# Decoder layer kernel: the residual stream in two halves that share their places with the weight buffers, and operands handed over mid-way

## The chip, the cores and the metric

The kernel runs on one core of a Trainium2 chip. The metric is the device time of one execution in microseconds (us). Five engines run side by side, each with its own queue: TensorE (PE, matmuls; its weight loads are shown as PEld), VectorE (DVE), ScalarE (ACT), GpSimd (POOL) and SyncE (SP, which here issues most DMAs; ACT issues the others).

## The reference

One decoder layer on 512 tokens of width 2048, in float32. A normalised input is projected for two groups of heads that work in parallel, a gated DeltaNet and a latent attention. Their outputs are concatenated, and the rest is what matters here:

```python
x = x + mixed @ w_out[l]
h = rms_norm(x, ffn_norm_w[l])
x = x + (jax.nn.silu(h @ w_gate[l]) * (h @ w_up[l])) @ w_down[l]
return rms_norm(x, final_norm_w)
```

`w_out` is 2048 x 2048, `w_gate` and `w_up` are 2048 x 5632, `w_down` is 5632 x 2048.

## The kernel before

Tokens are kept in four tiles of 128 partitions. Every matmul operand in float32 is split into a rounded high part and a low part (`hi` and `lo`), and `mm3` (L143) issues three matmuls for a product: high by high, high by low, low by high. `load_w` (L117) fetches a piece of weights, 512 KB, into one of two `raw` buffers on SP's queue, lets ACT cast it into `whi` (L137) and DVE subtract into `wlo` (L138); `whi` and `wlo` have three buffers each, unless the caller gives a destination of its own.

**Output projection.** `out_part` (L717) adds 512 columns of `mixed @ w_out` for four heads to `x2`, the residual stream (128 partitions x 4 token tiles x 2048 columns, 32 KB per partition): two `load_w`, then per token tile 12 matmuls of 512 columns and DVE's addition (L726). The last four calls (L889 to L894) also let ACT sum the squares of `x2` (L728), write `x2` to DRAM (`x2d`), and prepare what the next phase reads.

**Operands of the tokens.** `operands(i)` (L873) transposes 256 columns of `x2` on PE (8 transposes into two `bank` tiles of PSUM, L878), scales them on ACT (L882 to L884) into `stg`, of which there is one buffer, forms four differences on DVE (L886), and splits all seven into `ch` and `cl` (ACT L284, DVE L285). It runs eight times: 0 and 1 after block 1 of the last output projection, and so on, 6 and 7 at the end. Then the mean square is turned into `rstd` (POOL's power, L170), and `rows_of` (L239) spreads it over all partitions with matmuls (L150) into `rbc`.

**Gate and up.** For 22 pairs of feature tiles `unit` (L912) computes 256 columns of a product with 2048 inputs by Strassen-Winograd: seven `product`s of 24 matmuls of 256 columns each, once for `w_gate` and once for `w_up`. Its 2 MB of weights come by four DMAs into one of two `wraw` buffers (L916); DVE forms sums of their quarters (L927; three of them per unit in `raw` buffers, one in `sw`), and each product's weights are split into `whi` and `wlo`. The result `silu(gate) * up` goes to DRAM (`actd`), in 11 groups of four feature tiles.

**Down.** For each group g, `act_group(g)` (L982) loads its activations back by two `load_w` into `ah` and `al` (two buffers each), and `down` (L1002) adds four column blocks of 512 to `x2b` (L1012): two `load_w` and 48 matmuls of 512 columns per block. `act_group(g + 1)` is called ahead of `down(g)`. The last group runs by token tile instead, with its weights held in `fh` and `fl`, so that the final normalisation and the output can follow. Its DMAs for `x2b` (L999, 4 MB) and the final gain (L1000) are issued by ACT.

**Order and places.** Each engine runs its own instructions in the order emitted. The framework takes them in program order among those that are ready in its own model of the run, and puts in the waits. Tiles live in pools; a new tile waits for the last use of the tile whose slot it takes, or whose bytes lie under it after a pool was closed. Pools stack from two sides of the memory. On the right, `wr` (the `wraw` buffers) and `gu` (the results of units) open where `x2` and the operands of the output projection were, and reach far enough to lie over the closed pool `tr` of the left side (`stg`, `jo`); `ad` (`ah`, `al`) opens where `wr` was. `banks` (L99) does the same for the eight PSUM banks.

Of the kernel before, what the change touches and what calls it, by code (L numbers as in the profile page):

```python
# [89 lines left out]
def layer_kernel(ctx: ExitStack, tc: tile.TileContext, x, positions, w_in, a_log, dt_bias, w_uq, w_ukv,  # L90
# [605 lines left out]
    banks(op=1, score=3, acc=2, bank=2)  # L696
    x2_stack = right.enter_context(ExitStack())
    x2 = pool(x2_stack, "x2", side="right").tile([P, NT, D], F32, name="x2")
    mix_right = right.enter_context(ExitStack())
# [5 lines left out]
    for c in range(4):  # L705
        nc.scalar.dma_start(x2[:, :, c * S:(c + 1) * S], xv[:, :, c * S:(c + 1) * S])

# [8 lines left out]

    def out_part(k0, mg, c, jo=None):  # L717
        cs = slice(c * S, (c + 1) * S)
        ws = [load_w(w_out_v[:, k0 + 2 * kk:k0 + 2 * kk + 2, cs], 2, S) for kk in range(2)]
        for t4 in range(NT):  # L720
            sl = slice(t4 * P, (t4 + 1) * P)
            a = acc()
            for k in range(4):
                wh, wl = ws[k // 2]
                mm3(a, mg[0][:, k, sl], mg[1][:, k, sl], wh[:, k % 2, :], wl[:, k % 2, :], k == 0, k == 3)
            nc.vector.tensor_tensor(out=x2[:, t4, cs], in0=a, in1=x2[:, t4, cs], op=ALU.add)  # L726
            if jo is not None:
                nc.scalar.activation(jo, x2[:, t4, cs], AF.Square, accum_out=ssx[:, t4, c:c + 1])  # L728

# [143 lines left out]
    def operands(i):  # L873
        tps = []
        for k in (2 * i, 2 * i + 1):
            tp = bank()
            for t4 in range(NT):
                nc.tensor.transpose(tp[:, t4 * P:(t4 + 1) * P], x2[:, t4, k * P:(k + 1) * P], ident)  # L878
            tps.append(tp)
        st = tr.tile([P, N7, H], F32, name="stg", tag="stg", bufs=1)  # L880
        wa, wb = fw[:, 2 * i:2 * i + 1], fw[:, 2 * i + 1:2 * i + 2]
        nc.scalar.mul(st[:, 0, :], tps[0][:, 0:H], wa)  # L882
        nc.scalar.mul(st[:, 5, :], tps[0][:, H:S], wa)
        nc.scalar.mul(st[:, 1:3, :].rearrange("p a n -> p (a n)"), tps[1], wb)  # L884
        for o, x, y in ((3, 5, 0), (5, 2, 5), (4, 2, 3), (6, 1, 4)):
            nc.vector.tensor_tensor(out=st[:, o, :], in0=st[:, x, :], in1=st[:, y, :], op=ALU.subtract)  # L886
        split(ch[:, :, i, :], cl[:, :, i, :], st)

    for c in range(4):  # L889
        out_part(12, mg_b, c, jo)  # L890
        nc.scalar.dma_start(x2d[c].rearrange("p (t n) -> p t n", t=NT), x2[:, :, c * S:(c + 1) * S])
        if c:
            operands(2 * c - 2)
            operands(2 * c - 1)  # L894
# [5 lines left out]
    rsq(rstd, st4[:, 0:4])  # L900
    rows_of(tr, rstd, rbc, "jo")
    mix_right.close()
    x2_stack.close()
    tr_stack.close()
# [3 lines left out]
    gu = pool(gu_right, "gu", side="right")  # L908
    wr_right = right.enter_context(ExitStack())
    wr = pool(wr_right, "wr", bufs=2, side="right")  # L910
# [52 lines left out]

    for u in range(NFF // 2):
        g, o = divmod(u, 2)
        s = gu.tile([P, 2, S], F32, name="sg", tag="sg", bufs=2)
        unit(wg_v, u * 2 * P, s)
        nc.vector.tensor_tensor(out=s, in0=s, op=ALU.mult,
                                in1=rbc.rearrange("p (o n) -> p o n", o=1).broadcast_to([P, 2, S]))
        nc.scalar.activation(s, s, AF.Silu)  # L970
        t = gu.tile([P, 2, S], F32, name="up", tag="up")
        unit(wu_v, u * 2 * P, t)
        nc.vector.tensor_tensor(out=s, in0=t, in1=s, op=ALU.mult)
        nc.scalar.dma_start(actd[g].rearrange("p (k n) -> p k n", n=S)[:, 2 * o:2 * o + 2, :], s)


    wr_right.close()
    banks(bank=8)
    ad_right = right.enter_context(ExitStack())
    ad = pool(ad_right, "ad", bufs=2, side="right")  # L980
# [9 lines left out]

    cur = act_group(0)
    cb_stack.close()
# [21 lines left out]

    for g in range(NG - 1):
        nxt = act_group(g + 1)
        down(g, *cur)
        cur = nxt
    prev = cur
# [69 lines left out]
```

## Time and profile before

| What | Value |
|---|---|
| Time, median of 3 runs | 2510.67 us (2506.42 to 2512.49) |
| Profiled execution: its own time | 2509.5 us |
| Profiled execution: span from first to last instruction | 2507.7 us |
| PE busy | 2345.4 us, 94% of the span |
| DVE, ACT busy | 1565.9 us (62%), 899.6 us (36%) |
| Mean granted TensorE clock | 0.965 of full |
| Moved by DMA | 257.69 MB, mean 103 GB/s |

A duration of a matmul in the profile includes the time in which the next one already runs; the distance of two starts is what one costs. The order in time is output projection with operands up to about 1005 us, gate and up until 1905.6 us, down projection after that. A releaser, where one is shown, is what ended an engine's idle time, as far as the profile tells.

### The profile page before, as it was taken

Reading aid. Unit: us, or ns where it says so; the run is one execution under the profiler, and the core shown is the slowest. Engines: PE = TensorE matmul, PEld = TensorE weight load, DVE = VectorE, ACT = ScalarE, POOL = GpSimd, SP = SyncE. Lnnn points to the kernel's source line nnn. Section 1 sums busy time; section 2 is a strip of 40 time slices with the busy share of each in tenths; the row PEclk is TensorE's granted clock in tenths of the full one; section 3 lists DMA queues with packets and bytes.
Section 4 is the critical chain, followed back from the end, with each engine's and each line's share of the span. In section 5 each row is a group of like instructions: output and inputs, shape, how many; then the busy total and the mean of one; then the engine's idle time right before and its main releaser. Section 6 shows DMA issues by size and latency. Waiting matters only on the chain.

```text
span 2507.7 us, 35015 instructions
## 1 busy us (share of the span) xinstructions
PE 2345.4 (94%) x14310; PEld 2067.5 (82%) x14310; DVE 1565.9 (62%) x2248; ACT 899.6 (36%) x1435; POOL 83.4 (3%) x89
## 2 busy tenths in 40 slices
PE   8999999999999996799999999999997888788888
PEld 6778877777777785799999999999996777677776
DVE  6656565654655556677777777777774444444446
ACT  5333333332332335344444444444442111211123
POOL 0011111100000000000000000000000000000000
PEclk9999999999999997899999999999998999899999
DMA  5222322222322222433333333333335322333333
GB/s 172 78 71 81 83 79 78 76 77 69 129 80 72 64 69 82 143 110 118 110 119 122 130 118 119 119 110 118 110 118 181 95 94 92 101 109 101 94 100 118
DMA packets 210401, 257.69 MB, mean 103 GB/s; under 512 B 18112, under 2 KB 162752, under 8 KB 210112
## 3 DMA queue, kind: packets, MB, share of 16 engines
q1 hardware_dynamic: 197920, 225.55, 29.1%
q10 hardware_dynamic: 12320, 29.90, 3.3%
q8 instruction: 112, 1.84, 0.3%
q14 instruction: 49, 0.40, 0.1%
HBM read 235.23 MB, written 20.19 MB: 102 GB/s over the span
## 4 chain that ended last, share of the span: by engine, by line
PE 81%; DVE 7%; DMA 5%; ACT 3%; issue 2%; POOL 1%; ACTq 0%; SPq 0%; POOLq 0%; DVEq 0%
PE x L147 7%; PE x L145 7%; PE x L146 7%; PE acc L146 7%; PE acc L147 7%; PE acc L145 7%; PE bank L145 6%; PE bank L146 6%; PE bank L147 6%; PE bank L150 4%; PE y L147 3%; PE y L146 3%; PE y L145 3%; DMA raw<-in_w_down 2%; PE z L145 2%
## 5 line engine op out<-in xcount | busy, mean ns | idle before, releaser
L137 ACT CAST whi<-raw 128x1024 fp32r<-128x1024 f32 (+1 forms) x210 | 218.2, 1039 | 578.4 <-PE bank L147 233.5
L145 PE MATMUL x<-ch,whi 128*128 128x256 f32 x1408 | 399.4, 284 | 14.1 <-ACT whi L284 14.1
L146 PE MATMUL x<-cl,whi 128*128 128x256 f32 x1408 | 399.1, 283 | 0.0
L147 PE MATMUL x<-ch,wlo 128*128 128x256 f32 x1408 | 399.1, 283 | 0.0
L138 DVE TENSOR_TENSOR wlo<-raw,whi 128x1024 fp32r<-128x1024 f32 (+1 forms) x210 | 253.4, 1208 | 194.4 <-ACT whi L137 193.8
L145 PE MATMUL bank<-whi,ah 128*128 128x512 f32 x640 | 260.2, 410 | 80.4 <-ACT whi L137 80.4
L145 PEld LDWEIGHTS x<-ch,whi 128*128 128x128 f32 x1408 | 271.1, 193 | 14.5 <-ACT whi L284 14.4
L146 PEld LDWEIGHTS x<-cl,whi 128*128 128x128 f32 x1408 | 271.1, 193 | 0.0
L147 PEld LDWEIGHTS x<-ch,wlo 128*128 128x128 f32 x1408 | 271.0, 192 | 0.0
L146 PE MATMUL acc<-hl,whi 128*128 128x512 f32 (+1 forms) x656 | 263.7, 402 | 0.0
L145 PE MATMUL acc<-hh,whi 128*128 128x512 f32 (+1 forms) x656 | 261.7, 399 | 1.8 <-ACT whi L137 1.8
L147 PE MATMUL acc<-hh,wlo 128*128 128x512 f32 (+1 forms) x656 | 263.1, 401 | 0.0
L146 PE MATMUL bank<-wlo,ah 128*128 128x512 f32 x640 | 260.1, 406 | 0.4
L147 PE MATMUL bank<-whi,al 128*128 128x512 f32 x640 | 257.0, 402 | 0.0
L1012 DVE SCALAR_TENSOR_TENSOR x2b<-bank,rstd,x2b 128x512 f32<-128x512 f32 x160 | 119.9, 750 | 189.8 <-PE bank L147 189.8
L284 ACT CAST whi<-wraw 128x1024 fp32r<-128x1024 f32 x132 | 138.3, 1048 | 221.8 <-PE y L146 143.9
L145 PEld LDWEIGHTS bank<-whi,ah 128*128 128x128 f32 x640 | 125.7, 199 | 110.9 <-ACT whi L137 84.8
L284 ACT CAST whi<-raw 128x1024 fp32r<-128x1024 f32 x132 | 138.5, 1050 | 200.2 <-PE x L146 152.4
L146 PE MATMUL y<-cl,whi 128*128 128x256 f32 x704 | 199.2, 283 | 0.0
L147 PE MATMUL y<-ch,wlo 128*128 128x256 f32 x704 | 199.2, 283 | 0.0
L145 PE MATMUL y<-ch,whi 128*128 128x256 f32 x704 | 199.2, 283 | 0.0
L285 DVE TENSOR_TENSOR wlo<-wraw,whi 128x1024 fp32r<-128x1024 f32 x132 | 161.4, 1223 | 44.7 <-ACT whi L284 44.7
(320 smaller groups left out, 4478.5 us busy)
## 6 DMA issues: line engine op xcount, KB each, us to landing
wraw<-in_w_gate SPq DMA_DIRECT2D x88, 512.0 KB, 5.8
wraw<-in_w_up SPq DMA_DIRECT2D x88, 512.0 KB, 5.6
raw<-in_w_down SPq DMA_DIRECT2D x88, 512.0 KB, 3.8
raw<-in_w_in SPq DMA_DIRECT2D x80, 512.0 KB, 3.7
raw<-in_w_out SPq DMA_DIRECT2D x32, 512.0 KB, 3.8
actd<-sg ACTq DMA_DIRECT2D x22, 512.0 KB, 2.6
raw<-actd SPq DMA_DIRECT2D x22, 512.0 KB, 3.7
rep<-dr ACTq DMA_DIRECT2D x8, 512.0 KB
```

The lines of the kernel that those rows point to most:

```text
L137: nc.scalar.copy(hi[:, :k * n], raw[:, :k * n])
L138: nc.vector.tensor_tensor(out=lo[:, :k * n], in0=raw[:, :k * n], in1=hi[:, :k * n].bitcast(F32), op=ALU.subtract)
L145: nc.tensor.matmul(ps, lhsT=lh, rhs=rh, start=start, stop=False, skip_group_check=further)
L146: nc.tensor.matmul(ps, lhsT=lh, rhs=rl, start=False, stop=False, skip_group_check=further)
L147: nc.tensor.matmul(ps, lhsT=ll, rhs=rh, start=False, stop=stop, skip_group_check=further)
L150: nc.tensor.matmul(ps, lhsT=l, rhs=r, start=start, stop=stop)
L284: nc.scalar.copy(dst_h, src)
L285: nc.vector.tensor_tensor(out=dst_l, in0=src, in1=dst_h.bitcast(F32), op=ALU.subtract)
L1012: nc.vector.scalar_tensor_tensor(out=x2[:, t4, cs], in0=a, scalar=rstd[:, t4:t4 + 1], in1=x2[:, t4, cs], op0=ALU.mult, op1=ALU.add)
```

## The change

- `x2` becomes two tiles `x2h` of 1024 columns, 16 KB per partition each, in a pool `big` with two slots, `b0` and `b1`. `x2s` picks the right half for a slice of columns.
- These slots go on to hold the weights of `unit`: the gate units' in `b0`, the up units' in `b1`. The pool `wr` is gone.
- Then they hold the activations: `act_group(g)` takes one tile with `ah` and `al` in slot `b0` or `b1` by the parity of g. The pool `ad` is gone.
- `act_group(0)` is called ahead of the last up unit, `act_group(g + 1)` inside `down(g)` after two of its four blocks.
- `operands(2c - 2)` is called half-way through block c of the last output projection, after two of four token tiles, and `operands(2c - 1)` after the block as before.
- `rows_of` for `rbc` moves from before the first gate unit to behind it, with its temporary in `gu`.
- `gu` is closed ahead of the down projection.

```diff
-    x2 = pool(x2_stack, "x2", side="right").tile([P, NT, D], F32, name="x2")
+    big = pool(right, "big", side="right")
+    x2h = [big.tile([P, NT, D // 2], F32, name=f"x2{h}", tag=f"b{h}") for h in range(2)]
...
-            nc.vector.tensor_tensor(out=x2[:, t4, cs], in0=a, in1=x2[:, t4, cs], op=ALU.add)
+            xs2 = x2s(t4, cs)
+            nc.vector.tensor_tensor(out=xs2, in0=a, in1=xs2, op=ALU.add)
             if jo is not None:
-                nc.scalar.activation(jo, x2[:, t4, cs], AF.Square, accum_out=ssx[:, t4, c:c + 1])
+                nc.scalar.activation(jo, xs2, AF.Square, accum_out=ssx[:, t4, c:c + 1])
+            if t4 == 1 and halfway is not None:
+                halfway()
...
     for c in range(4):
-        out_part(12, mg_b, c, jo)
+        out_part(12, mg_b, c, jo, (lambda: operands(2 * c - 2)) if c else None)
...
         if c:
-            operands(2 * c - 2)
             operands(2 * c - 1)
     operands(6)
     operands(7)
...
-    rows_of(tr, rstd, rbc, "jo")
...
-    def unit(w_v, c0, dst):
-
-        raw = wr.tile([P, KD, 2 * P], F32, name="wraw", tag="wraw")
+    def unit(w_v, c0, dst, buf):
+
+        raw = big.tile([P, KD, 2 * P], F32, name="wraw", tag=buf)
...
     def act_group(g):
-        ah = ad.tile([P, 4, S], F32R, name="ah", tag="ah")
-        al = ad.tile([P, 4, S], F32R, name="al", tag="al")
+        a = big.tile([P, 2, 4, S], F32R, name="ag", tag=f"b{g % 2}")
+        ah, al = a[:, 0], a[:, 1]
...
-    cur = act_group(0)
+    for u in range(NFF // 2):
+        g, o = divmod(u, 2)
+        s = gu.tile([P, 2, S], F32, name="sg", tag="sg", bufs=2)
+        unit(wg_v, u * 2 * P, s, "b0")
+        if u == 0:
+            rows_of(gu, rstd, rbc, "dg")
...
+        t = gu.tile([P, 2, S], F32, name="up", tag="up")
+        if u == NFF // 2 - 1:
+            cur = act_group(0)
+        unit(wu_v, u * 2 * P, t, "b1")
...
     def down(g, ah, al):
+        nxt = None
         for c in range(4):
+            if c == 2:
+                nxt = act_group(g + 1)
...
+        return nxt
 
     for g in range(NG - 1):
-        nxt = act_group(g + 1)
-        down(g, *cur)
-        cur = nxt
+        cur = down(g, *cur)
```

## Rows read from the trace of the kernel before

**Rows 1.** The page, part 2: busy tenths in 40 equal slices of the span.

```profile
PE   8999999999999996799999999999997888788888
...
PEclk9999999999999997899999999999998999899999
```

**Rows 2.** Busy time by stretch: length; PE, PEld, DVE, ACT, POOL; clock, DMA share, GB/s.

```profile
972.00:1017.00 45.00, 10.44 (x45) 7.86 (x43) 22.82 (x36) 18.11 (x24) 1.01 (x1) 0.54 0.30 100
1017.00:1905.56 888.56, 888.56 (x7390) 888.38 (x7390) 686.07 (x660) 392.79 (x507) 0.00 (x0) 1.00 0.35 116
1905.56:1937.80 32.24, 15.86 (x51) 11.98 (x50) 9.62 (x10) 6.29 (x8) 0.00 (x0) 0.68 0.75 267
1970.20:2023.87 53.67, 46.53 (x193) 37.54 (x192) 23.59 (x26) 10.40 (x11) 0.00 (x0) 0.90 0.31 98
```

**Rows 3.** Waits from 1905 to 2508 us: total us, times, longest us.

```profile
ACT ah L137 <- PE bank L146: 98.6, 9, 11.0
...
PE bank L145 <- ACT whi L137: 80.4, 11, 11.2
```

**Rows 4.** Timeline of ACT, down projection: start, duration, operation [idle before <- releaser].

```profile
1970.21 1.99 ACT L137 CAST ah<-raw 128x1024 fp32r<-128x1024 f32 x2 [10.96 <-PE bank L146]
1976.40 1.04 ACT L137 CAST whi<-raw 128x1024 fp32r<-128x1024 f32 x1 [4.20 <-DMA raw<-in_w_down]
...
2000.97 1.05 ACT L137 CAST whi<-raw 128x1024 fp32r<-128x1024 f32 x1 [8.46 <-PE bank L147]
...
2011.85 1.05 ACT L137 CAST whi<-raw 128x1024 fp32r<-128x1024 f32 x1 [8.46 <-PE bank L147]
...
2398.83 1.99 ACT L137 CAST ah<-raw 128x1024 fp32r<-128x1024 f32 x2 [10.96 <-PE bank L146]
```

**Rows 5.** Timeline of PE after a group of the down projection.

```profile
1977.50 1.22 PE L145 MATMUL bank<-whi,ah 128*128 128x512 f32 x2 [7.10 <-ACT whi L137]
```

**Rows 6.** DMA landing of raw (after 1880 us) and of x2b.

```profile
DMA to landing us min/median/max: 3.5/3.7/9.2
...
DMA to landing us min/median/max: 9.4/12.5/15.5
```

**Rows 7.** Timeline of DVE around the last gate unit.

```profile
1873.48 1.22 DVE L927 TENSOR_TENSOR raw<-wraw 128x1024 f32<-128x1024 f32 x1
...
1875.88 1.22 DVE L285 TENSOR_TENSOR wlo<-raw,whi 128x1024 fp32r<-128x1024 f32 x1
```

**Rows 8.** Timelines of PE, ACT and SP where the down projection begins.

```profile
1916.92 1.65 PE L145 MATMUL bank<-whi,ah 128*128 128x512 f32 x3 [11.20 <-ACT whi L137]
...
1937.79 1.06 ACT L137 CAST whi<-raw 128x1024 fp32r<-128x1024 f32 x1 [0.30 <-PE bank L147]
...
1893.57 9.54 SPq L135 DMA_DIRECT2D raw<-actd  x4
```

**Rows 9.** Timelines of ACT, DVE and SP ahead of the first gate unit.

```profile
998.96 0.47 ACT L882 ACTIVATE stg<-bank,vec 128x256 f32<-128x256 f32 x1 [2.15 <-DVE cl L285]
...
1014.91 2.00 ACT L284 CAST whi<-wraw 128x1024 fp32r<-128x1024 f32 x2 [11.52 <-DMA wraw<-in_w_gate]
...
1003.43 2.02 DVE L285 TENSOR_TENSOR cl<-stg,ch 128x1792 fp32r<-128x1792 f32 x1 [0.78 <-ACT ch L284]
...
1005.84 2.02 SPq L916 DMA_DIRECT2D wraw<-in_w_gate  x4
```

**Rows 10.** Timeline of PE from the output projection to the first gate unit.

```profile
946.67 1.03 PE L878 MATMUL bank<-fst,x 128*128 128x128 f32 x8
...
953.12 0.60 PE L878 MATMUL bank<-fst,x 128*128 128x128 f32 x4
...
1016.01 0.58 PE L145 MATMUL x<-ch,whi 128*128 128x256 f32 x1 [14.09 <-ACT whi L284]
...
1021.45 0.28 PE L147 MATMUL z<-ch,wlo 128*128 128x256 f32 x1
```

**Rows 11.** Groups by line, 972 to 1017 us: count, busy us, mean ns, idle before.

```profile
L150 PE MATMUL bank<-dg,cst 128*128 128x128 f32 x8 | 2.1, 441 | 4.6 <-ACT stg L883 4.6
```

More of the change, by code (lines that the diff above doesn't have):

```diff
@@ L696, in layer_kernel, with x2s @@
     banks(op=1, score=3, acc=2, bank=2)
-    x2_stack = right.enter_context(ExitStack())
-    x2 = pool(x2_stack, "x2", side="right").tile([P, NT, D], F32, name="x2")
+    big = pool(right, "big", side="right")
+    x2h = [big.tile([P, NT, D // 2], F32, name=f"x2{h}", tag=f"b{h}") for h in range(2)]
+    def x2s(t, k):
+        h = k.start // (D // 2)
+        return x2h[h][:, t, k.start - h * (D // 2):k.stop - h * (D // 2)]
+    every = slice(0, NT)
     mix_right = right.enter_context(ExitStack())
@@ L705, in layer_kernel @@
     for c in range(4):
-        nc.scalar.dma_start(x2[:, :, c * S:(c + 1) * S], xv[:, :, c * S:(c + 1) * S])
+        nc.scalar.dma_start(x2s(every, slice(c * S, (c + 1) * S)), xv[:, :, c * S:(c + 1) * S])
     def mix_group(slot):
@@ L715, in gdn_group, with out_part @@
         return mh, ml
-    def out_part(k0, mg, c, jo=None):
+    def out_part(k0, mg, c, jo=None, halfway=None):
         cs = slice(c * S, (c + 1) * S)
@@ L877, in operands @@
             for t4 in range(NT):
-                nc.tensor.transpose(tp[:, t4 * P:(t4 + 1) * P], x2[:, t4, k * P:(k + 1) * P], ident)
+                nc.tensor.transpose(tp[:, t4 * P:(t4 + 1) * P], x2s(t4, slice(k * P, (k + 1) * P)), ident)
             tps.append(tp)
@@ L889, in layer_kernel @@
     for c in range(4):
-        out_part(12, mg_b, c, jo)
-        nc.scalar.dma_start(x2d[c].rearrange("p (t n) -> p t n", t=NT), x2[:, :, c * S:(c + 1) * S])
+        out_part(12, mg_b, c, jo, (lambda: operands(2 * c - 2)) if c else None)
+        nc.scalar.dma_start(x2d[c].rearrange("p (t n) -> p t n", t=NT),
+                            x2s(every, slice(c * S, (c + 1) * S)))
         if c:
-            operands(2 * c - 2)
             operands(2 * c - 1)
@@ L900, in layer_kernel @@
     rsq(rstd, st4[:, 0:4])
-    rows_of(tr, rstd, rbc, "jo")
     mix_right.close()
-    x2_stack.close()
     tr_stack.close()
@@ L908, in layer_kernel @@
     gu = pool(gu_right, "gu", side="right")
-    wr_right = right.enter_context(ExitStack())
-    wr = pool(wr_right, "wr", bufs=2, side="right")
-    def unit(w_v, c0, dst):
-        raw = wr.tile([P, KD, 2 * P], F32, name="wraw", tag="wraw")
+    def unit(w_v, c0, dst, buf):
+        raw = big.tile([P, KD, 2 * P], F32, name="wraw", tag=buf)
         for kk in range(4):
@@ L962, in unit @@
         nc.scalar.copy(dst[:, 1, 0:H], X)
[L964 to L980, printed above, removed]
     def act_group(g):
-        ah = ad.tile([P, 4, S], F32R, name="ah", tag="ah")
-        al = ad.tile([P, 4, S], F32R, name="al", tag="al")
+        a = big.tile([P, 2, 4, S], F32R, name="ag", tag=f"b{g % 2}")
+        ah, al = a[:, 0], a[:, 1]
         v = actd[g].rearrange("p (k n) -> p k n", n=S)
@@ L989, in act_group @@
         return ah, al
-    cur = act_group(0)
+    for u in range(NFF // 2):
[4 more added lines that the diff above has]
+            rows_of(gu, rstd, rbc, "dg")
+        nc.vector.tensor_tensor(out=s, in0=s, op=ALU.mult,
+                                in1=rbc.rearrange("p (o n) -> p o n", o=1).broadcast_to([P, 2, S]))
+        nc.scalar.activation(s, s, AF.Silu)
+        t = gu.tile([P, 2, S], F32, name="up", tag="up")
+        if u == NFF // 2 - 1:
+            cur = act_group(0)
+        unit(wu_v, u * 2 * P, t, "b1")
+        nc.vector.tensor_tensor(out=s, in0=t, in1=s, op=ALU.mult)
+        nc.scalar.dma_start(actd[g].rearrange("p (k n) -> p k n", n=S)[:, 2 * o:2 * o + 2, :], s)
+    banks(bank=8)
+    gu_right.close()
     cb_stack.close()
```

## The prediction

> **What bounds the kernel now.** The page's 40 slices come first [rows 1]: PE is at 9 tenths nearly everywhere, with two kinds of holes, slices 16 and 17 and then the last ten at 7 to 8 tenths, and the granted clock dips in four of these. So TensorE is the bound, and only what opens a gap in it matters. The busy time by stretch [rows 2] separates the stages that the change touches. From 972 to 1017 us PE has 10.4 of 45 us of work; from 1017 to 1905.6 it is full at clock 1.00 (7390 matmuls in 888.6 us, 0.120 us each); from 1905.6 to 1937.8 it has half; and one group of the down projection (1970.2 to 2023.9) leaves 7 of 53.7 us idle, at a mean granted clock of 0.90, that is, a part of it at 1.2 instead of 2.4 GHz.
>
> The waits name the last of these [rows 3]. Nine times ACT's cast into ah waits for PE, 98.6 us in all, and PE in turn waits for ACT's whi, 80.4 us in 11 waits. ACT's timeline shows the circle [rows 4]: act_group(g+1) stands ahead of down(g), and its ah is the buffer that down(g-1) reads to its last matmul. Until then its two loads keep both raw buffers, so no weight of the new group can be loaded. After the casts at 1970.21 comes a weight load, its cast at 1976.40, and PE starts at 1977.50 after 7.10 us of nothing [rows 5].
>
> **The down projection, the main term.** Within a group a column block takes 2011.85 - 2000.97 = 10.88 us [rows 4], 48 matmuls without a gap, so four are 43.52 us. From the first cast into ah after a group to the ninth is 2398.83 - 1970.21 = 428.62 us, eight groups of 53.58 us [rows 4]. Each boundary costs 10.06 us: 7.1 us of idleness and 2.9 us because PE then runs at its low clock for a while. With nine boundaries that is 90.5 us. The change fetches act_group(g+1) after two blocks of down(g), into the place of group g-1, which by then has been dead for about 22 us, so the casts wait for nothing but their own data.
>
> What takes its place? The same ten loads per group, two of them now between blocks 1 and 2. A raw buffer is busy for one landing, a cast and a subtraction: about 3.7 us [rows 6] + 1.05 us [rows 4] + 1.2 us [rows 7], some 6.2 us with the hand-offs. Two buffers and ten loads make 5 x 6.2 = 31 us, less than the 43.5 us of matmuls. Followed through a group that starts at T: act loads land at about T+6 and T+12 (one raw buffer is held until T+11.8 by a weight that waits for its whi), block 2's weights at T+15.5 and T+18. Block 2 starts at T+21.8. If the raw buffers alternate strictly, the last of these slips to T+21.5 and PE waits some 0.7 us. I bound the new mid-group cost between 0 and 7 us over nine groups (more is a rival) and take 3, nearer to 0 because the first reading leaves 3 to 5 us of slack. The last group's weights keep their time: what comes before them is ten loads either way.
>
> **Into the down projection.** The last product of the last unit ends at 1905.56, PE starts again at 1916.92 after 11.20 us [rows 8], waits a second time, and ends block 0 at 1937.79, where the cast into its freed whi starts [rows 8]; without gaps it would end at 1905.56 + 10.88 = 1916.44. That is 21.3 us lost. Four act loads stood in the raw buffers ahead of the first weights; SP spread them over 9.5 us from 1893.57 [rows 8]. Now the two of act_group(0) go before the last up unit and those of act_group(1) after block 1, so the first weights take those early raw places, are cast by about 1903, and PE goes straight on. Left over: the 4 MB of x2b, which land 9.4 to 15.5 us after issue [rows 6] and are issued by ACT in one piece, ahead of casts, at the same point as before. Block 1's second weight and block 2's weights, behind act_group(1), pay for that. I estimate 8 us lost, so a gain of 13.3, with bounds of 6 (block 2 waits as long as PE did at first, and the clock falls) and 21 (no wait).
>
> **Into the gate and up phase.** The chain of operands(0) to (7) has one stg buffer and alternates between ACT and DVE; the last runs from 998.96 to 1003.43 + 2.02 = 1005.45 [rows 9]. Then SP issues the first gate weights (1005.84), ACT gets them at 1014.91 [rows 9], PE starts at 1016.01 and, slow at first, is through product 1 at 1021.45 [rows 10]. The weights waited for places that the operands' temporaries and x2 occupy. In the new kernel the first gate unit's buffer is the half of x2 with columns 0 to 1023, free after operands(3), and its 2 MB land while operands(4) to (7) run; SP has nothing else to issue there. Its first cast and subtraction fit into ACT's and DVE's pauses in that chain. What remains is the chain, and it starts earlier: operands(0)'s transposes come at 946.67, right behind block 1's matmuls [rows 10]; half a block earlier is 5.4 us. Work queued behind them, the adds and squares of the block's other half, has a PE 30 us ahead of the chain's end to hide behind. So operands(7) ends near 1000 us, and product 1 ends three matmuls later, at about 1000.7. Product 2 then loses some 2 us to the low clock. Against 1021.45 that is 18 us. Bounds: 9 (no earlier start, casts only after operands(7)) and 21 (all of it, no low clock); I take 18, since each step has its cover in the rows.
>
> **The rest.** rows_of now stands between unit 0's halves: 2.1 us for its 8 matmuls in the low-clock stretch [rows 11], about 1 us at full clock, on PE's path, where before PE was idle anyway: +1. Its DVE work, and the squares and x2 copies through other views, have the same sizes as before: 0, hidden by PE. In the last up unit the act loads hold both raw buffers until the gate unit's last split; but the sums that need them are made early. The first of them ran at 1873.48 [rows 7], while its first use, product 3, starts at 1905.56 - 5 x 24 x 0.120 = 1891.2. Some 10 us later is still in time: 0.
>
> **The SP queue there.** In program order act_group(0)'s loads come ahead of the last up unit's weights. SP's row shows that a load that waits for raw holds the queue: four issues in 9.5 us [rows 8]. I still take 0, since the emitted order is not the program's: four transposes of operands(1), which lack a bank, appear at 953.12 with the next block's matmuls moved ahead of them [rows 10], and the up weights' buffer is free a whole unit ahead, long before a raw one is. The Trainium skill, "DMA: Bandwidth & Descriptors", section on the anatomy of one DMA, says that a DMA's semaphore wait happens on the issuing sequencer, before dispatch. By that rule alone, in program order, the weights would come late, and the sum would be 5 us smaller; it is a rival below.
>
> **Sum.** -90.5 + 3 - 13.3 - 18 + 1 = -117.8 us. The profiled execution took 2509.5 us, a span of 2507.7 and 1.8 around it, 1.2 under the median of the runs (2510.67). On the median: 2393 us.
>
> **Rivals.**
> (a) A new gap at block 2 of every group: both raw buffers are held when its weights are due. A gap of 3 us in nine groups is 27 us, so about 2417; if the clock falls each time (2.9 us more), 2443. For it: every whi waits for a raw buffer. Against: 31 us of raw work in 43.5. 14%.
> (b) The start brings only 9 us, because casts and sums put into the operand chain delay it, or the scheduler starts operands(0) no earlier: 2402. 10%.
> (c) The queue: SP keeps program order at the last up unit. The second act load issues when a raw is freed, at 1877.1 by the subtraction that frees it [rows 7], some 8 us before that unit's first product (1885.4), and 2 MB take 9.1 us (1005.84 to 1014.91, [rows 9]), so product 1 and its lo part come late by 5 us: 2398. This is the rule of the page named above. 10%.
> (d) The hand-over does not come loose, because the shared place counts as free only late: the boundaries stay, and only the two ends gain: 2393 + 87.5 = 2480. Against: the place was last read a group earlier. 2%.
> (e) Slower: the raw ring becomes the bound. If loads that follow each other closely land like the slowest one seen, 9.2 us instead of 3.7 [rows 6], a group takes 5 x (9.2 + 2.4) = 58 us instead of 53.6, 40 us over nine groups; with the ends gaining nothing under the same slow loads the time is 2550. It decides from a landing of about 8.3 us on. Against: 9.2 occurred beside the x2b loads, and one group moves only 98 GB/s [rows 2]. 3%.
> The forecast keeps 60%, and 1% lies where amounts cancel.
>
> **Numbers.** A measurement of this kernel can tell 0.3%, some 7.5 us, from no change. Faster by more: the forecast, (a) to (d), 96%; slower 3%; same 1%. The range takes the bounds of the sum's terms and (b), (c) and the milder half of (a): 2376 (start 21, entry 21, mid-group 0, and a little beyond) to 2426.
>
> **What would show it.** Right: the nine waits of ACT's ah for PE gone, groups of 43.5 to 44.5 us at clock near 1.00, first gate weights issued before 975, PE's first product done near 1001, PE idle under 2 us at the end of the last unit. Wrong: a PE wait for whi at a block other than 0 in every group, the first unit after 1008, or a gap at about the start of the last up unit. The forecast as a whole falls if the group period stays above 48 us.

## The result and the profile after

The changed kernel takes 2398.23 us (median; 2395.82 to 2402.94) where the kernel before takes 2510.57 us on the same chip (2506.42 to 2512.49): a ratio of 0.9557, 95% interval [0.9538, 0.9576], 112 us or 4.4% faster. Forecast were 2393 us, with a range of 2376 to 2426.

The profiled execution took 2397.31 us, with a span of 2395.5 us (2507.7 before) and a mean granted clock of 0.987 (0.965). PE is busy for 2320.1 us, 97% of the span (94%). The page's slices, to be laid beside [rows 1]:

```profile
PE   8999999999999999699999999999999999999998
...
PEclk9999999999999999799999999999999999999999
```

The holes of the last ten slices are gone, and of slices 16 and 17 one is left. Busy time by stretch, with the columns of [rows 2]: the start of gate and up, gate and up, the first group of the down projection, and a later group.

```profile
972.00:1017.00 45.00, 25.46 (x112) 21.44 (x111) 30.01 (x43) 21.92 (x30) 1.01 (x1) 0.71 0.28 93
1017.00:1897.58 880.58, 880.58 (x7334) 880.44 (x7334) 680.39 (x655) 391.73 (x504) 0.00 (x0) 1.00 0.35 117
1897.58:1948.93 51.35, 46.70 (x195) 37.76 (x194) 22.77 (x26) 10.78 (x11) 0.00 (x0) 0.93 0.62 215
1980.21:2023.73 43.52, 43.52 (x193) 36.04 (x192) 23.23 (x26) 10.54 (x10) 0.00 (x0) 1.00 0.39 121
```

PE fills the whole group at clock 1.00; before, a group took 53.6 us, at 0.90. Two holes remain: PE has 25.5 of 45 us of work at the start, and 46.7 of 51.4 us in the first group. ACT's timeline in the down projection, against [rows 4]:

```profile
1980.21 1.05 ACT L137 CAST whi<-raw 128x1024 fp32r<-128x1024 f32 x1 [7.67 <-PE bank L147]
...
1999.86 1.05 ACT L137 CAST ag<-raw 128x1024 fp32r<-128x1024 f32 x1 [6.36 <-DMA raw<-actd]
...
2005.92 1.05 ACT L137 CAST ag<-raw 128x1024 fp32r<-128x1024 f32 x1 [2.90 <-DMA raw<-actd]
...
2023.73 1.05 ACT L137 CAST whi<-raw 128x1024 fp32r<-128x1024 f32 x1 [7.63 <-PE bank L147]
```

The period is 2023.73 - 1980.21 = 43.52 us, four blocks of 10.88. The casts into the activations' place (`ag`, `ah` before) no longer wait for PE, but for their own data, while PE runs on. The waits from 1897 us to the end show it in sum, against [rows 3]:

```profile
ACT whi L137 <- PE bank L147: 189.3, 55, 8.5
ACT ag L137 <- DMA raw<-actd: 90.7, 20, 7.0
```

90.7 us of waiting, about what the nine waits for PE made before, and after the first group none of it is on PE's path: ACT has nothing to do in that time.

**Where the 112.2 us of span went.** Four marks in each trace give the parts: U, the start of DVE's last addition of block 0 in the last output projection (936.89 before, 938.93 after); DVE's sum `sg<-x,p` in unit 0, which says that PE is past its first products (1033.00, 1025.03); the end of the last product of the last unit (1905.56, 1897.58); the end of group 0 of the down projection.

| Part | forecast, us | traces, us |
|---|---|---|
| up to U, not touched by the change (scatter, see below) | 0 | +2.0 |
| start of gate and up: 96.1 to 86.1 from U to the sum, `rows_of` included | -17 | -10.0 |
| gate and up, last unit included: 872.6 both times | 0 | 0.0 |
| entry into down: lost in group 0, 21.1 to 7.8 | -13.3 | -13.3 |
| nine boundaries, and the cost mid-group | -87.5 | -90.5 |
| not placed | | -0.4 |
| span | -117.8 | -112.2 |

### The profile page after: what moved, and what is told of

It is laid out like the page before. It is cut to its first block, busy times and chain, and to the rows that moved or that the text cites. A ratio compares the mean times of both kernels' runs of the same rounds, so it can differ in the third digit from the quotient of the medians.

```text
span 2395.5 us, 34998 instructions
## 1 busy us (share of the span) xinstructions
PE 2320.1 (97%) x14310; PEld 2055.4 (86%) x14310; DVE 1561.1 (65%) x2248; ACT 901.3 (38%) x1435; POOL 83.4 (3%) x89
## 4 chain that ended last, share of the span: by engine, by line
PE 84%; DVE 7%; DMA 4%; ACT 2%; issue 2%; POOL 1%; ACTq 0%; SPq 0%; POOLq 0%; DVEq 0%
PE acc L146 7%; PE acc L147 7%; PE acc L145 7%; PE x L146 7%; PE x L145 7%; PE x L147 7%; PE bank L146 6%; PE bank L147 6%; PE bank L145 6%; PE bank L150 4%; PE y L146 3%; PE y L145 3%; PE y L147 3%; PE z L147 2%; PE z L146 2%; PE z L145 2%
## 5 line engine op out<-in xcount | busy, mean ns | idle before, releaser
L145 PE MATMUL bank<-whi,ag 128*128 128x512 f32 x640 | 249.7, 391 | 4.2 <-ACT whi L137 4.2
L146 PE MATMUL bank<-wlo,ag 128*128 128x512 f32 x640 | 250.1, 391 | 0.5 <-DVE wlo L138 0.5
L147 PE MATMUL bank<-whi,ag 128*128 128x512 f32 x640 | 249.7, 390 | 0.0
L285 DVE TENSOR_TENSOR wlo<-raw,whi 128x1024 fp32r<-128x1024 f32 x132 | 161.4, 1223 | 30.2 <-ACT whi L284 26.7
```

The source lines that it names most:

```text
L145: nc.tensor.matmul(ps, lhsT=lh, rhs=rh, start=start, stop=False, skip_group_check=further)
L146: nc.tensor.matmul(ps, lhsT=lh, rhs=rl, start=False, stop=False, skip_group_check=further)
L147: nc.tensor.matmul(ps, lhsT=ll, rhs=rh, start=False, stop=stop, skip_group_check=further)
L285: nc.vector.tensor_tensor(out=dst_l, in0=src, in1=dst_h.bitcast(F32), op=ALU.subtract)
```

## The experiments

The theory at this point, **A**: three independent parts, boundaries (some 91 us, from the point at which `act_group(g + 1)` is called), entry (13) and start (10), and the start fell short because unit 0's sums and splits were put into the operand chain, where DVE waits in order for the first weights. The rivals are in the expectations. Ratios are to the kernel before on the same chip; the runs are on several chips, on which the kernel before took 2507.85 to 2510.71 us, so differences of two medians are good to a few us. Where a run differs by a few us only, its median can't settle it: profiles reach U between 933.8 and 943.0 us, though all kernels have the same instructions in the same order up to there. So the start is read from marks in the trace, as distances from U.

### The boundaries: the late call alone, and the late call undone

On the kernel before:

```diff
     def down(g, ah, al):
+        nxt = None
         for c in range(4):
+            if c == 2:
+                nxt = act_group(g + 1)
...
+        return nxt
     for g in range(NG - 1):
-        nxt = act_group(g + 1)
-        down(g, *cur)
-        cur = nxt
+        cur = down(g, *cur)
```

> The kernel before with one part of the change alone: act_group(g + 1) is called after two blocks of down(g) instead of ahead of it; x2, the weight buffers, the pool ad with its two places and operands stay as before. Theory A (the boundaries come from the point of the call, not from the shared places): 9 boundaries of 10.06 us go, 90.5, and at the entry act_group(1)'s two loads no longer stand ahead of the first weights, which gives 3 to 10 more: 2510.6 - 94 to - 101 = 2410 to 2417. Rival (the hand-over needs the shared places, since ah and al of the pool ad come free too late): less than half of it, 2465 or more.

Measured: 2408.1 us (2406.51 to 2412.74), ratio 0.9594 [0.9578, 0.961]; the kernel before took 2509.17 us there, and 2509.17 - 2408.1 = 101.1 us is what theory A had at most. On the changed kernel, the other way round:

```diff
-            if c == 2:
+            if c == 0:
                 nxt = act_group(g + 1)
```

> The changed kernel, but act_group(g + 1) stands ahead of down(g) again (after none of its four blocks instead of after two). Theory A: each group period goes back from 43.5 to 53.6 us and the entry loses 3 to 10 us: 2398.2 + 90.5 + 3 to 10 = 2492 to 2499. Rival (the shared places are what frees the boundaries): below 2440.

Measured: 2488.41 us (2487.56 to 2489.49), ratio 0.9917 [0.9902, 0.9931], 90.2 us more than the changed kernel. First the waits of ACT in the kernel with the late call alone, from 1908 us on, then the timeline of ACT in the kernel with the call undone:

```profile
ACT whi L137 <- PE bank L147: 201.3, 60, 8.5
ACT ah L137 <- DMA raw<-actd: 84.1, 20, 6.6
```

```profile
1948.51 1.99 ACT L137 CAST ag<-raw 128x1024 fp32r<-128x1024 f32 x2 [11.18 <-PE bank L147]
...
2377.25 1.99 ACT L137 CAST ag<-raw 128x1024 fp32r<-128x1024 f32 x2 [11.18 <-PE bank L147]
```

In the first, the casts into `ah` of the old pool wait for their data and never for PE. In the second the old wait is back, nine casts with eight periods between them, (2377.25 - 1948.51) / 8 = 53.59 us each against 53.58 before. So the shared places have no part in the boundaries: the point of the call alone brings 90 of the 112 us, and the old pool `ad` with its two places would have done. What the call undone did not cost is the entry: 0 instead of the 3 to 10 expected. `act_group(0)` is there still called early and its loads are done during the last up unit, so that only the two of `act_group(1)` stand right ahead of the first weights, and its group 0 loses 1948.51 - 1897.46 - 43.52 = 7.5 us, like the changed kernel's.

### The entry: act_group(0) late again

```diff
-        if u == NFF // 2 - 1:
-            cur = act_group(0)
         unit(wu_v, u * 2 * P, t, "b1")
...
+    cur = act_group(0)
```

> The changed kernel, but act_group(0) is called behind the last up unit, as before, instead of ahead of it. Theory A (the entry gains because the first weights of the down projection find the raw buffers free): two act loads stand ahead of block 0's weights again, and PE waits at the start of the down projection: 4 to 8 us more, 2402 to 2406. Rival (it is only act_group(1) that mattered, and two act loads hide behind the last up unit's products wherever they are called): 2398.

Measured: 2398.46 us (2394.73 to 2400.31), ratio 0.9556 [0.9542, 0.957]: by the times the rival's "no difference", which the scatter of the runs (some 5 us) doesn't tell from a few us. The trace can. SP's issues and PE's waits of this run where the down projection begins:

```profile
1885.89 3.22 SPq L135 DMA_DIRECT2D raw<-actd  x2
1891.90 9.32 SPq L135 DMA_DIRECT2D raw<-in_w_down  x4
1903.89 12.15 SPq L135 DMA_DIRECT2D raw<-actd  x2
```

```profile
1899.62 0.50 PE L145 MATMUL bank<-whi,ag 128*128 128x512 f32 x1 [0.19 <-ACT whi L137]
1900.88 0.50 PE L146 MATMUL bank<-wlo,ag 128*128 128x512 f32 x1 [0.76 <-DVE wlo L138]
...
1926.10 1.59 PE L145 MATMUL bank<-whi,ag 128*128 128x512 f32 x4 [4.75 <-ACT whi L137]
```

Two act loads ahead of the first weights cost PE under 1 us at block 0, and the weights of block 2 come later behind the other two. Group 0 ends at 1952.13 and lost 1952.13 - 1897.88 - 43.52 = 10.7 us, against 7.8 in the changed kernel. In the kernel with the late call alone it lost 13.2 us, and there the first weights are issued 3.9 us ahead of the end of the last product (1904.65 and 1908.56), instead of 6.0 here (1891.90 and 1897.88). So taken in this order, 7.9 of the entry's 13.3 us come from `act_group(1)`, which the late call takes out of the way of the first weights (21.1 - 13.2), 2.5 from what else the change does there (13.2 - 10.7), and 2.9 from calling `act_group(0)` early. The shares hold for this order only: with `act_group(0)` early, `act_group(1)` ahead of the first weights cost nothing (7.5 us lost with the call undone, above). With two act loads right ahead of the first weights PE waits under 1 us at block 0 in all three kernels (0.95 here, 0.86 with the late call alone, 0.78 with the call undone), with the four of before 11.20 [rows 8]. Theory A's 4 to 8 us for calling `act_group(0)` late were too many.

### The entry: what is left of it

```diff
-    for c in range(4):
-        nc.scalar.dma_start(x2[:, :, c * S:(c + 1) * S], x2d[c].rearrange("p (t n) -> p t n", t=NT))
-    nc.scalar.dma_start(fin, final_norm_w...)
+    def x2b_block(c):
+        nc.scalar.dma_start(x2[:, :, c * S:(c + 1) * S], x2d[c].rearrange("p (t n) -> p t n", t=NT))
+    x2b_block(0)
...
+                if g == 0 and t4 == 0:
+                    n = (c + 1) * S
+                    if c < 3:
+                        nc.vector.tensor_copy(x2[:, 0, n:n + 1], x2[:, 0, n - 1:n])
+                        x2b_block(c + 1)
+                    else:
+                        nc.vector.tensor_copy(fin[:, 0:1], x2[:, 0, n - 1:n])
+                        nc.scalar.dma_start(fin, final_norm_w...)
```

The one-column copy makes each load depend on the addition before it.

> The changed kernel, but the four loads of x2b (1 MB each, a block of columns) and that of the final gain are no longer issued at once: each is issued when the first addition of the block before it is done. Theory A (the 7.8 us that the entry into the down projection still loses are block 2's weights landing beside 5 MB of other loads): the two waits of PE at block 2, 4.65 us, go, and with them the 3 us at the low clock; 2398.2 - 5 to 8 = 2390 to 2393. Rival (the loss only moves: now a block's first addition waits for its own part of x2b, and DVE's subtractions stand behind it): 2397 or more.

Measured: 2389.26 us (2388.27 to 2391.51), ratio 0.953 [0.9514, 0.9546] against 0.9557 [0.9538, 0.9576] for the changed kernel. The intervals overlap a little, so the traces have to show what it is worth. In the changed kernel, PE's waits in group 0 and the busy time around them (columns as in [rows 2]):

```profile
1923.72 0.79 PE L145 MATMUL bank<-whi,ag 128*128 128x512 f32 x1 [4.18 <-ACT whi L137]
1924.98 0.79 PE L146 MATMUL bank<-wlo,ag 128*128 128x512 f32 x1 [0.47 <-DVE wlo L138]
```

```profile
1906.00:1914.00 8.00, 8.00 (x37) 6.63 (x36) 4.39 (x6) 1.71 (x2) 0.00 (x0) 1.00 0.99 376
1914.00:1922.00 8.00, 5.53 (x25) 4.25 (x23) 2.73 (x3) 0.40 (x1) 0.00 (x0) 1.00 1.05 399
1922.00:1930.00 8.00, 5.82 (x14) 4.26 (x15) 3.68 (x4) 3.14 (x3) 0.00 (x0) 0.57 0.52 184
```

All 16 DMA engines are busy from 1906 to 1922 us, at 376 to 399 GB/s, and block 2's weights have to pass among the 5 MB of x2b and the final gain. Their issue on SP and their cast on ACT, in the changed kernel and then in the experiment:

```profile
1913.65 19.19 SPq L135 DMA_DIRECT2D raw<-in_w_down  x5
1922.62 1.04 ACT L137 CAST whi<-raw 128x1024 fp32r<-128x1024 f32 x1 [8.22 <-DMA raw<-in_w_down]
```

```profile
1912.87 23.04 SPq L135 DMA_DIRECT2D raw<-in_w_down  x7
1918.47 1.05 ACT L137 CAST whi<-raw 128x1024 fp32r<-128x1024 f32 x1 [7.37 <-DMA raw<-in_w_down]
```

ACT itself spends 5.8 us on issuing the five loads in the changed kernel, which could have been the cause as well, but the first weights of block 2 are not issued earlier without it: 16.1 us after the first matmul of group 0 there, 16.7 us in the experiment. From issue to cast they take 9.0 us there and 5.6 us here, and that is most of the gain. In the experiment one wait is left, and DVE's row shows what it hangs on:

```profile
1912.89 0.69 PE L146 MATMUL bank<-wlo,ag 128*128 128x512 f32 x1 [1.83 <-DVE wlo L138]
```

```profile
1908.92 1.41 DVE L1022 SCALAR_TENSOR_TENSOR x2b<-bank,rstd,x2b 128x512 f32<-128x512 f32 x2 [3.75 <-DMA x2b<-x2d]
...
1911.63 1.21 DVE L138 TENSOR_TENSOR wlo<-raw,whi 128x1024 fp32r<-128x1024 f32 x1
```

Group 0 loses 1943.65 - 1896.14 - 43.52 = 4.0 us instead of 7.8. Theory A holds for the cause, not for the full size: 3.8 of 5 to 8 us. The remainder is the rival's mechanism in small: the first addition waits for its part of x2b, and the subtraction that PE needs stands behind it on DVE (in the changed kernel too such an addition waits 3.23 us, and the raw buffer for block 2's weights comes free behind it).

### The start: four cuts at the operand chain

The four edits to the changed kernel are: `operands(2c - 2)` again behind the block;

```diff
-        out_part(12, mg_b, c, jo, (lambda: operands(2 * c - 2)) if c else None)
+        out_part(12, mg_b, c, jo)
...
+            operands(2 * c - 2)
             operands(2 * c - 1)
```

> The changed kernel, but operands(2c-2) is again called behind block c instead of half-way through it. Theory A (the start fell short of its 18 us because unit 0's sums and splits were emitted into the operand chain and DVE waits there in order for the first weights): the chain begins half a block, 5.4 us, later, and ends up to 5.4 us later: 2398.2 + 4 to 6 = about 2403. Rival R1 (the half-way hand-over itself slows the chain, because its work mixes with the other half-block's additions and squares): as fast as the changed kernel or faster, 2392 to 2398. Rival R2 (the shortfall comes from upstream of the chain): 2398.

the places swapped;

```diff
-        a = big.tile([P, 2, 4, S], F32R, name="ag", tag=f"b{g % 2}")
+        a = big.tile([P, 2, 4, S], F32R, name="ag", tag=f"b{(g + 1) % 2}")
...
-        unit(wg_v, u * 2 * P, s, "b0")
+        unit(wg_v, u * 2 * P, s, "b1")
...
-        unit(wu_v, u * 2 * P, t, "b1")
+        unit(wu_v, u * 2 * P, t, "b0")
```

> The changed kernel with the two places swapped: gate units in b1 (columns 1024 to 2047 of x2, read by operands(4) to (7)), up units in b0, activations by the other parity. The first gate weights can land only after operands(7), so none of unit 0's work can enter the chain. Theory A: the chain takes the 57.6 us it took before instead of 66.7 and ends near 1001.5, then 2 MB of weights, casts and the first product follow as before (16 us from the chain's end to the end of product 1): product 1 ends near 1017.5 instead of 1011.1, time about 2404. Rival R1 (half-way hand-over slows the chain): the chain stays at 66 to 67 us, ends near 1010.6, product 1 ends near 1026.6, time about 2413. Rival R2 (upstream): chain as in R1, 2413.

x2 cut into other halves;

```diff
-        h = k.start // (D // 2)
-        return x2h[h][:, t, k.start - h * (D // 2):k.stop - h * (D // 2)]
+        c = k.start // S
+        h, o = ((1, 0), (0, 0), (0, S), (1, S))[c]
+        return x2h[h][:, t, k.start - c * S + o:k.stop - c * S + o]
```

> The changed kernel, but the halves of x2 are cut differently: b0 holds columns 512 to 1535 (blocks 1 and 2), b1 holds blocks 0 and 3. operands(i) follow the columns in the same order, so b0 is free after operands(5) instead of operands(3), about 13 us later, and the first gate weights land that much later. Theory A: DVE's first sum no longer stands ahead of a late landing in operands(3), the chain loses its extra 9 us or most of it, product 1 ends 5 to 9 us earlier: 2389 to 2394. Rivals R1 and R2: the chain keeps its 66.7 us, 2397 to 2400; if the weights then come too late, up to 2405.

and these other halves without the half-way call.

> x2 cut so that b0 holds blocks 1 and 2 (no work of unit 0 in the operand chain), and operands(2c-2) again called behind block c instead of half-way. Theory B (half-way, the chain starts some 5 us earlier but then takes 3 to 4 us longer, since DVE's additions of the other half-block, which wait for PE in order, stand between the operands' differences; what is left was used up by unit 0's work): the chain ends 1.5 to 3 us later than with the half-way call, 2396 to 2398. Rival 1 (the half-way call is worth its whole half block): 2399 to 2400. Rival 2 (it is worth nothing): 2394 to 2395.

Measured: 2398.67 us, ratio 0.9559 [0.9545, 0.9572]; 2394.22, 0.9542 [0.9528, 0.9556]; 2394.56, 0.9542 [0.9528, 0.9555]; 2392.88, 0.9547 [0.9529, 0.9565]. No two of these intervals are apart, nor from the changed kernel's, so the marks decide; theory A's 2403 for the first was a miss all the same. The columns are distances from U in us: ACT's scaling of 512 columns (L884 before, L894 after) in the first, sixth and last `operands`, and the sum `sg<-x,p`.

| Kernel | U at | first | sixth | last | sum |
|---|---|---|---|---|---|
| before | 936.89 | 12.3 | 49.6 | 62.8 | 96.1 |
| changed | 938.93 | 6.3 | 52.7 | 65.9 | 86.1 |
| not half-way | 939.32 | 12.3 | 52.5 | 65.6 | 84.8 |
| places swapped | 938.60 | 6.3 | 47.0 | 60.2 | 82.9 |
| other halves | 936.79 | 6.3 | 47.0 | 63.3 | 83.2 |
| other halves, not half-way | 933.79 | 12.3 | 49.4 | 66.6 | 86.8 |

How exact this is: three kernels above with the same start of gate and up as the changed one (call undone, `act_group(0)` late, x2b by need) have last scalings at 65.8 to 66.0 and sums at 85.0 to 86.5.

The sixth scaling sorts the theories. It comes at 47.0 with the half-way call and none of unit 0's work ahead of it, at 49.5 with neither (before, and other halves not half-way), and at 52.6 with unit 0's work, half-way or not. The last scaling can't be used so: with the other halves unit 0's work is not out of the chain, as one expectation has it, but further back in it, and the last circle takes 9.2 and 9.1 us instead of 6.6. So **half-way** a chain that starts 6.0 us earlier keeps 2.5 of it; and **unit 0's work**, in the chain, costs 52.7 - 47.0 = 5.7 us with the half-way call and 52.5 - 49.5 = 3.0 without. In the kernel as changed the second eats the first, and the half-way call brings nothing (1.3 us on the wrong side in the sum, less than equal starts differ by). Three stretches of DVE's rows in the changed kernel show both:

```profile
954.87 0.42 DVE L896 TENSOR_TENSOR stg<-stg 128x256 f32<-128x256 f32 x1
956.31 0.69 DVE L734 TENSOR_TENSOR x<-acc,x 128x512 f32<-128x512 f32 x1 [1.02 <-PE acc L147]
956.92 1.21 DVE L896 TENSOR_TENSOR stg<-stg 128x256 f32<-128x256 f32 x3
...
969.25 0.69 DVE L734 TENSOR_TENSOR x<-acc,x 128x512 f32<-128x512 f32 x1 [2.03 <-PE acc L147]
969.86 2.02 DVE L285 TENSOR_TENSOR cl<-stg,ch 128x1792 fp32r<-128x1792 f32 x1
...
975.66 1.23 DVE L933 TENSOR_TENSOR raw<-wraw 128x1024 f32<-128x1024 f32 x1 [2.99 <-DMA wraw<-in_w_gate]
976.80 0.42 DVE L896 TENSOR_TENSOR stg<-stg 128x256 f32<-128x256 f32 x1
977.13 1.22 DVE L933 TENSOR_TENSOR raw<-wraw 128x1024 f32<-128x1024 f32 x1
978.27 0.75 DVE L896 TENSOR_TENSOR stg<-stg 128x256 f32<-128x256 f32 x2
```

In the first two, additions of the other half-block stand between a chain's differences, and before its last subtraction, and wait there for PE's accumulator. (The kernel before has such waits too, of 1.10 us at 951.03 for one, and no run takes these additions out of the chain: that they are what takes back 3.5 of the 6.0 us is read from the rows and not shown by an experiment.) In the last, unit 0's sum of weights stands ahead of the differences of `operands(3)`, whose first scaling came at 971.97, and DVE waits 2.99 us for the weights; the next sum and, further on, two subtractions of 1.22 us follow. The first scaling of the next `operands` comes 12.4 us after this one's (984.33); the last four follow each other at 6.6.

The rival "half-way slows the chain" is thus right for most of what half-way should bring, "upstream" stands for no more than the 2.0 us up to U, and theory A holds for its part and not for the whole. Its price for the swapped places was wrong: 2404 expected, 2394.22 measured, since it let the weights wait for the chain's end. They don't:

```profile
994.41 2.02 SPq L922 DMA_DIRECT2D wraw<-in_w_gate  x4
```

```profile
1003.74 0.58 PE L145 MATMUL x<-ch,whi 128*128 128x256 f32 x1 [9.40 <-ACT whi L284]
```

This is SP's and PE's row of that kernel. The second half of x2 is free when PE has transposed it, before the last `operands` is even scaled (998.80), and PE has its first weights before the last subtraction into `cl` ends (1004.57). In the kernel before the issue came after that subtraction (1005.84, [rows 9]), since by the layout of the pools the weights' buffer lay over `stg` too. So what the change brings at the start is that 2 MB land beside the chain; how early they do is of no use, and too early does harm.

For the last pair, other halves with and without half-way, the medians are equal where 2 us more were expected without. The kernel without reached U 3.0 us earlier; from U on, its last scaling is 3.3 us later and its sum 3.6. That is a little more than theory B's 1.5 to 3 and less than the whole half block, and it is hidden in the total.

### A shorter chain, and all together

```diff
         nc.scalar.mul(st[:, 0, :], tps[0][:, 0:H], wa)
-        nc.scalar.mul(st[:, 5, :], tps[0][:, H:S], wa)
...
+        nc.scalar.mul(st[:, 5, :], tps[0][:, H:S], wa)
...
-        split(ch[:, :, i, :], cl[:, :, i, :], st)
+        split(ch[:, 0:3, i, :], cl[:, 0:3, i, :], st[:, 0:3, :])
+        split(ch[:, 3:7, i, :], cl[:, 3:7, i, :], st[:, 3:7, :])
```

> The changed kernel, but each operands(i) splits its seven pieces in two steps: the three that need only ACT's scaling first, then the four that are mostly DVE's differences (the order of ACT's three scalings changes with it). ACT's first cast then runs beside DVE's differences, and the 6.6 us that one operands takes by its single stg buffer should fall to 4.5 to 5.5. Theory A with a chain bound by the one stg buffer's circle: the four operands at the end save 1 to 2 us each, 4 to 8 us in all, 2390 to 2394. Rival R3 (the chain is bound by the order in which DVE meets the first weights, not by the circle): 2396 to 2400, no gain.

Measured: 2396.14 us (2394.66 to 2398.69), ratio 0.9549 [0.9536, 0.9563]; last scaling at 62.9 from U, sum at 82.9. The circle of one `operands` is 6.31 us, not 4.5 to 5.5:

```profile
994.37 1.22 DVE L896 TENSOR_TENSOR stg<-stg 128x256 f32<-128x256 f32 x3 [1.54 <-ACT stg L894]
995.51 0.95 DVE L285 TENSOR_TENSOR cl<-stg,ch 128x768 fp32r<-128x768 f32 x1
996.38 0.42 DVE L896 TENSOR_TENSOR stg<-stg 128x256 f32<-128x256 f32 x1
997.91 1.23 DVE L285 TENSOR_TENSOR cl<-stg,ch 128x1024 fp32r<-128x1024 f32 x1 [1.12 <-ACT ch L284]
```

The cast of the first piece does run beside the differences, but its subtraction (0.95 us) was put ahead of the fourth difference and so onto the path. A miss in size. Of the 3.0 us by which the last scaling is earlier from U, 0.6 are the two last circles and 0.4 the new place of the scaling of 512 columns; the circle before these two takes 7.15 us, 0.55 more than in the changed kernel, with a sum of unit 0 in it, and the rest, 2.6, falls among the first five operands, where unit 0's work lies otherwise.

This kernel had reached U at 943.0, the latest of all, so it was profiled again.

> The kernel with operands split in two pieces once more, unchanged. It reached U (DVE's last addition of block 0 in the last output projection) at 943.0 us, where the changed kernel and five of its variants reached it at 938.4 to 939.3, though up to there all have the same instructions in the same order. If that offset belongs to the kernel (the places of its tiles or its code), U comes at 942.4 to 943.6 again; if it is scatter of the execution, it comes nearer to 938 to 939, and the 2.0 us between the kernels before and after mean nothing.

Measured: 2393.64 us (a single run); U at 938.95, the last scaling 62.9 from it as before, the sum at 82.7. The offset at U is scatter of the execution. The distances from U hold: 62.90 and 62.89, 82.9 and 82.7.

> The two edits together on the changed kernel: x2 cut so that b0 holds blocks 1 and 2, and each operands(i) split in two steps. Theory A: no unit work ahead of operands(6) and a shorter circle add up, the chain ends 8 to 14 us earlier than in the changed kernel: 2384 to 2390. Rival (once the chain is shorter, the 2 MB of weights that start only after operands(5) set the start): no more than the better of the two edits alone.

Measured: 2389.45 us (2386.84 to 2392.91), ratio 0.9523 [0.9509, 0.9537], below the changed kernel's interval. The last scaling comes at 59.5 from U, the sum at 79.5, 6.6 us ahead of the changed kernel; 3.7 us more were there at U already.

> Three edits on the changed kernel: x2 cut so that b0 holds blocks 1 and 2, operands split in two steps, x2b loaded block by block. Theory A: start and entry are independent of each other, so the entry's 5 to 8 us come on top of the 2389.5 of the first two edits: 2381 to 2385. Rival as for the edit of x2b alone: 2388 or more.

Measured: 2382.5 us (2378.62 to 2384.49), ratio 0.9502 [0.9484, 0.9519]. It is the fastest and beats both kernels. Its sum comes at 78.1 from U, and group 0 of the down projection loses 1933.70 - 1887.11 - 43.52 = 3.1 us, 4.7 less than in the changed kernel. The sum is 8.0 us earlier than there, so by the marks start and entry add up.

## Why the prediction was right, and where it wasn't

The main term, four fifths of the gain, was right by its mechanism. That the total is only 5.6 us off is in part luck: the start brought 7.0 us less than its term, and 3.0 us set aside for mid-group were not needed. That the time comes out at rival (c)'s 2398 is chance, since (c) did not come about.

**The boundaries (-90.5): right, to the tenth.** 10.06 us for each of nine came out of the periods in one view, and undoing the call alone gives 90.2 us back. The mechanism was right too: two loads waiting for a buffer that PE still reads, and all weights behind them. That the place of the activations is shared plays no part in it.

**Mid-group (+3, 0 to 7): 0.** After the first group PE has no wait until the last group, and the period is 43.52. The nearer reading, with 3 to 5 us of slack, was the right one. Rivals (a) and (e) fall with it: raw lands after 3.5 to 8.6 us, 3.6 in the median (1897 us to the end).

**Entry (-13.3): right in size, right in what stays.** 7.8 us are lost where 8 were estimated, and at block 2, beside the loads of x2b. The clock falls there, as it was said for the lower bound. The prediction gave both act groups credit for it; once `act_group(1)` is out of the way, calling `act_group(0)` early is worth 2.9 us of it, and with `act_group(0)` early the place of `act_group(1)` is worth nothing. In [rows 8] PE waited 11.20 us, now it waits 4.18 and 0.47.

**Start (-18, bounds 9 to 21): the term that was mis-sized, -10.0 with `rows_of`'s 1 in it.** It is close to rival (b), by the first of (b)'s two mechanisms (the second did not come about: the first scaling is 6.0 us earlier). Two sentences failed. "Work queued behind them, the adds and squares of the block's other half, has a PE 30 us ahead of the chain's end to hide behind": it hid from PE, but on DVE it stands within the chain, and the 6.0 us of earlier start shrink to 2.5, for this reason as far as the rows tell. "Its first cast and subtraction fit into ACT's and DVE's pauses in that chain": it is two sums and two subtractions, the first sum with a wait of 2.99 us for its weights, and the chain is 5.7 us longer by it. Both together make the chain's last scaling 3.1 us later from U than before (65.9 against 62.8) where it was to be 5.4 earlier, a loss of 8.5; 1.5 of it come back by the term's rounding and behind the chain's end. (The Trainium skill, "TensorE: Matmul & The Clock Gate", on the architecture of the array, calls DVE's and ACT's queues strictly first in, first out; the 2.99 us agree.) Behind the chain's end the working was right: product 1 ends in the changed kernel some 0.7 us after the last subtraction of the operands, and before it took 16 ([rows 9, 10]). DVE's last subtraction and PE's last rows of the first two products (`x`, `z`), which here run side by side:

```profile
1008.60 2.02 DVE L285 TENSOR_TENSOR cl<-stg,ch 128x1792 fp32r<-128x1792 f32 x1 [1.80 <-ACT ch L284]
```

```profile
1011.06 0.42 PE L147 MATMUL x<-ch,wlo 128*128 128x256 f32 x1
...
1011.49 0.41 PE L147 MATMUL z<-ch,wlo 128*128 128x256 f32 x1
```

Of the signs on record, the groups of 43.52 us, the first gate weights issued ahead of 975 (964.50) and the end of the last unit without a gap on PE came as forecast. Product 1, forecast near 1001, ended at 1011.3, and with it came one of the signs of being wrong, the first unit after 1008.

**The last up unit and SP's queue (0): right.** SP's rows of the changed kernel:

```profile
1851.33 3.08 SPq L922 DMA_DIRECT2D wraw<-in_w_up  x4
1865.49 3.33 SPq L135 DMA_DIRECT2D raw<-actd  x2
```

The last up unit's weights are issued ahead of the act loads, though the program calls them the other way round, and gate and up takes the same 872.6 us. So rival (c) did not come about. The Trainium skill's rule for it ("DMA: Bandwidth & Descriptors", anatomy of one DMA: the semaphore wait is on the issuing sequencer) isn't touched by this; the order that it needs was never emitted.

**Rival (d)** fell at the first group: no cast of `ag` waits for PE, and undoing the call with the shared places kept brings the old wait back. **Not in the sum:** the +2.0 us up to U. They lie within the scatter of single executions, 938.95 and 943.0 us for one and the same kernel.

## What to carry to other kernels

A prefetch that must wait for a buffer still in use, called ahead of the work whose inputs share its staging buffers, stops all of them: call it where its place has long been free, and look at the period from group to group to know what it costs. Before counting on work "beside" a chain, write the chain out on each of its engines in order: an instruction that waits there, for an accumulator or for a load, stops the whole chain, and an earlier load can make it worse. Where a term ends at a phase of large loads, issue these in the order in which they are needed.

## What the runs showed of the hardware that was not expected

How much a load is held up by others: with the loads of x2b and the final gain issued at once, the weights of the down projection landed after 6.3 us in the median (five loads, 1900 to 1935 us), with x2b by need after 4.8 (six loads), against 3.6 in the whole of the down projection. And the clock behind short waits. In the changed kernel PE stood still for 4.18 us, and the granted clock was 0.57 from 1922 to 1930 us, most of that time at the level of 1.2 GHz. In the kernel with x2b by need it stood still for 1.83 us, and the next 8 us were granted 0.79; in the fastest kernel it stood still for 1.50 us, and the clock stayed at 1.00. The busy time of the first, then the wait and the busy time of the second:

```profile
1905.00:1913.00 8.00, 6.17 (x28) 4.80 (x26) 4.25 (x8) 2.10 (x2) 0.00 (x0) 1.00 0.62 216
1913.00:1921.00 8.00, 8.00 (x29) 6.42 (x30) 3.98 (x6) 1.53 (x2) 0.00 (x0) 0.79 0.71 255
```

```profile
1903.53 0.50 PE L146 MATMUL bank<-wlo,ag 128*128 128x512 f32 x1 [1.50 <-DVE wlo L138]
```

```profile
1901.00:1905.00 4.00, 2.50 (x11) 1.77 (x10) 3.61 (x5) 1.05 (x1) 0.00 (x0) 1.00 0.59 165
1905.00:1909.00 4.00, 4.00 (x19) 3.31 (x18) 1.47 (x3) 0.00 (x0) 0.00 (x0) 1.00 0.96 335
```

A wait as short as 1.83 us was not expected to cost anything at the clock; it cost 0.21 x 8 = 1.7 us more, about as much again, and the one of 1.50 us cost nothing more.
